# The router's two half-width products of a pair of channel blocks, side by side on TensorE's columns, with four places for x1

## The chip, the core and the metric

The kernel runs on one core of a Trainium2 chip. The metric is the device time of one execution in microseconds (us), as a median of several runs. The core's engines are PE (TensorE: matrix products), DVE (VectorE), ACT (ScalarE), POOL (GpSimd) and SP (SyncE, which here mostly issues transfers); PEld in the views is PE's loading of the stationary operand.

## What is computed

One layer of a decoder trunk over 2048 tokens of 1024 channels: a convolution module as token mixer, then a mixture of 32 gated-MLP experts, of which each token takes two, chosen by a router. Cut to what the change touches:

```
h   = rmsnorm(x, g1) * (1 + sc1) + sh1
u   = a * sigmoid(gt)            where a, gt = split(h @ w_in + b_in)
y   = silu(layernorm(depthwise_conv31(u) + b_dw)) @ w_out
x   = x + gate1 * y                                    # "x1" in the kernel
h   = rmsnorm(x, g2) * (1 + sc2) + sh2
grp_logits = h @ w_rg + b_rg     # 4 groups
exp_logits = h @ w_re + b_re     # 32 experts         -> 36 columns: "the router"
x   = x + gate2 * sum over the two chosen experts of p_e * (silu(h @ w_gate[e]) * (h @ w_up[e])) @ w_down[e]
out = rmsnorm(x, g3)
```

The kernel takes the router's products from the un-normalised x1 and applies the norm's factor afterwards to the 36 sums of each token (`finish`), so that the router can run while x1 is still being made, block of channels by block of channels.

## The kernel before, in words

**Tiling.** The 2048 tokens are cut into four chunks c = 0 to 3 of 512 tokens (`NCH`), the 1024 channels into eight blocks j = 0 to 7 of 128 (`KD`). The convolution's output product works on five pieces (`PIECES`): chunks 0, 1 and 2 whole, chunk 3 in two halves of 256 tokens. Channels lie on the 128 partitions and tokens along the free axis until the router is done; then the rows are written out by token, gathered by expert, and the experts run.

**Steps.** A loop over s = 8c + j issues for each step the input product of chunk c, block j (`conv_in`, 2 x 24 products of 128x128 by 512), the depthwise convolution of the block before (`dw`: some taps as column-tiled products on PE, L461, some on DVE, L490, some on ACT and POOL, L478 and L484), the layer norm of the chunk before (`layer_norm`), and, at the places that `PACE` gives, the output product of the chunk before (`conv_out`). The two halves of chunk 3 come at the end, all of `conv_out` of the one and then of the other, while the first expert's weights are being loaded. What is written is only a set of priorities: the order of each engine's instructions is set when the program is built, by a planner that runs a timeline of its own estimates, takes what is ready and prefers what is marked urgent. Each engine then works through its own list strictly in that order, and so does SP's list of transfers: a transfer whose place in memory isn't free yet holds all that stand behind it.

**conv_out (L542 to L562), one block j of one piece.** It takes a place for x1 and starts the load of the residual block into it (L548, 128 x 512 or 128 x 256 float32), runs 24 products into a PSUM bank (`gemm`, L388 to L390), adds the gated result to x1 on DVE (L552), transposes x1 on PE (L555), copies the transposed block out (L557 or L559), and runs the router's product of this block (L561): `wr2[:, j, :]`, 128 x 64 float32, as the stationary operand, x1 as the moving one. Even j accumulate in partitions 0 to 63 of the bank `lg`, odd j in partitions 64 to 127, so that each uses one half of PE's columns (`tile_position=(0, g)`). A float32 product of this kind stands in the trace as two records.

**Places.** x1 has two places in chunks 0 to 2 (`TMPB["x1"]`, 128 x 2 KB each), shared with the scratch tiles `junk`, `ls` and `zt` of `prep_norm`, `finish` and `mod_g2` (`JT`). In the two pieces of chunk 3 x1 takes its places from the pool "prod" instead (`X1E`), which has three. A place comes free when the router's product has read it.

**After the last block** `finish` copies `lg` out on ACT, adds the two halves on PE (L581, with the stacked identity `two`), and `routing` makes the choice; then come the experts (`Step`, L1111 and L1113).

Of the kernel before, what the change touches and what calls it, by code (L numbers as in the profile page):

```python
# [24 lines left out]
KD = D // P  # L25
# [69 lines left out]
MAXQ = max(q for t in TAPS for q, _ in t)  # L95
RW = CH + 4 * (MAXQ - 1)
WPB, WRB, UPB = 8, 1, 4
TMPB = {"acc2": 2, "prod": 3, "x1": 2}
BANKS = {"po": 1, "pa": 1, "pg": 1, "tr": 2, "lg": 1, "acc": 1, "out": 1}
LAG_DW, LAG_LN, LAG_OUT = 1, 2, 3  # L100
DELAY = 1
# [27 lines left out]
def moe_kernel(ctx, tc, x, xT, cols, ada, fing, w_in, w_out, b_r, wgu, wd, out):  # L129
    nc = tc.nc  # L130
# [76 lines left out]
    def pool(name, bufs=1, stack=None, **kw):  # L207
        return (stack or p1).enter_context(tc.tile_pool(name=name, bufs=bufs, reuse_waits="tile", **kw))
# [6 lines left out]
    grp = [pool("grp1")]  # L215
    sp = {tag: pool("sp_" + tag, n) for tag, n in TMPB.items() if tag != "x1"}
    rt4 = pool("rt4")
# [6 lines left out]

    sp["x1"] = pool("sp_x1", TMPB["x1"])
    mp = pool("mp")
# [7 lines left out]
    wr2 = c1.tile([P, KD, 64], F32, name="wr2")  # L234
# [13 lines left out]
    def urgent(offset=URGENT):  # L248
        return tc.high_priority(offset=offset)
# [4 lines left out]
    def bank(tag, name):  # L254
        return ps[tag].tile([P, 512], F32, tag=tag, name=name)

    def tmp(tag, name, shape=(P, 512), dt=F32):
        return sp[tag].tile(list(shape), dt, tag=tag, name=name)
# [85 lines left out]
    def parts(a):  # L344
        return a.rearrange("p (i q) -> p i q", q=P)
# [19 lines left out]
    def w_unit(c, src, dst, priority=WPRI, kept=0):  # L365

        with urgent(priority):
            h = wp.tile([P, D], F32R, tag="w", name="wh")
            l = wp.tile([P, D], F32R, tag="w", name="wl")
            if c <= kept:  # L370
                r = raw("wraw", src.tensor.name == w_in.tensor.name and c < 2)
                nc.sync.dma_start(r[:], src)
                S.activation(h[:], r[:], AF.Copy)
                V.tensor_tensor(l[:], r[:], h[:].bitcast(F32), op=OP.subtract)
                if c == kept:
                    nc.scalar.dma_start(dst[0], h[:].bitcast(F32))
                    nc.scalar.dma_start(dst[1], l[:].bitcast(F32))
            else:
                nc.sync.dma_start(h[:].bitcast(F32), dst[0])
                nc.sync.dma_start(l[:].bitcast(F32), dst[1])  # L380
            return h, l

    def gemm(po, w, xx, n):
        for k in range(KD):
            xh, xl = xx[k]
            wh, wl = (w[m][:, k * P:(k + 1) * P] if len(w) == 2 else w[2 * m + k // 4][:, k % 4 * P:(k % 4 + 1) * P]
                      for m in range(2))
            nc.tensor.matmul(po[:, :n], wh, xh[:, :n], start=(k == 0), stop=False)  # L388
            nc.tensor.matmul(po[:, :n], wh, xl[:, :n], start=False, stop=False)  # L389
            nc.tensor.matmul(po[:, :n], wl, xh[:, :n], start=False, stop=(k == KD - 1))  # L390
# [144 lines left out]
    def conv_out_tiles(c, o, n):  # L535
# [3 lines left out]
            xr = group("xr", 1)[:, :n // P, :]  # L539
        return xr, bank("lg" if o == 0 else "acc", "lg")  # L540

    def conv_out(c, o, n, j, z, xr, lg):  # L542

        end = c == NCH - 1
        w = wlast[j] if end else w_unit(c, w_out[j], (wo_d[0, j], wo_d[1, j]))
        x1 = tmp(X1E if end else "x1", "x1")
        with urgent(X1P):
            nc.sync.dma_start(x1[:, :n], xT[j][:, T0[c] + o:T0[c] + o + n])  # L548
        po = bank("pa" if end and j % 2 else "po", "po")
        gemm(po, w, z, n)  # L550
        with urgent():
            V.scalar_tensor_tensor(x1[:, :n], po[:, :n], modc[:, 16 + j:17 + j], x1[:, :n], op0=OP.mult, op1=OP.add)  # L552
            pb = bank("pg" if end and j % 2 else "out", "x1_t")
            for i in range(n // P):
                nc.tensor.transpose(pb[:, i * P:(i + 1) * P], x1[:, i * P:(i + 1) * P], ident[:])  # L555
            if j < XRV[c]:
                V.tensor_copy(xr[:, :, j * P:(j + 1) * P], parts(pb[:, :n]))  # L557
            else:
                S.activation(xr[:, :, j * P:(j + 1) * P], parts(pb[:, :n]), AF.Copy)  # L559
            g = 64 * (j % 2)  # L560
            nc.tensor.matmul(lg[g:g + 64, :n], wr2[:, j, :], x1[:, :n], start=(j < 2), stop=(j >= KD - 2),  # L561
                             tile_position=(0, g))  # L562

    def finish(c, o, n, xr, lg):

# [238 lines left out]
    def part(piece, j):  # L804
        conv_out(*piece, j, zs[piece], *outs[piece])
        if j == KD - 1:
            n = PIECES.index(piece)
            with urgent(FINISH[n]):
                L = finish(*piece, *outs[piece])
            with urgent(ROUTE[n]):  # L810
                return routing(*piece, L)
# [9 lines left out]
    for s in range(NS + LAG_OUT):  # L821
        c, j = divmod(s, KD)
# [47 lines left out]
    for m in g2t:  # L870
        w, n = P // m, D // m
# [478 lines left out]
```

## Time and profile before

| what | value |
|---|---|
| runs shown | 1604.31, 1604.81, 1607.11 us; median 1604.81 us |
| the profiled execution's own time | 1602.93 us |
| its span (first to last instruction) | 1601.2 us |
| PE busy | 1469.0 us, 92% of the span |
| DVE busy | 1120.2 us, 70% |
| ACT busy | 973.9 us, 61% |
| POOL busy | 741.2 us, 46% |
| DMA | 455.99 MB, 285 GB/s on average |
| granted TensorE clock, mean | 0.965 |

The share of an engine over the whole span is a mean over stages with different limits. The convolution fills about the first 800 us and the experts the rest. Busy times of PE are a union of records that overlap: the distance from one start to the next says more of a product's cost than its duration. "issue" as what ended an idle time means that the profile shows nothing that the engine waited for.

### The profile page before, as it was taken

What the parts mean: (1) busy time and instruction counts of PE and PEld (TensorE: products, weight loads), DVE (VectorE), ACT (ScalarE), POOL (GpSimd) and SP (SyncE); (2) the same over time, 40 slices, a digit from 0 to 9 for tenths busy, and PEclk for the clock granted to TensorE, in tenths of its full rate; (3) what the DMA queues carried; (4) which work ended last, traced back from release to release, by engine and by line L of the source; (5) the groups of instructions that cost most, each with busy time, mean ns of one, the idle gap of its engine ahead of it and who ended that gap; (6) DMA issues with size and microseconds to landing.
All of it is one profiled execution on the core that took longest, in us unless ns stands there. A gap on an engine that the chain in (4) does not pass through costs nothing.

```text
span 1601.2 us, 24058 instructions
## 1 busy us (share of the span) xinstructions
PE 1469.0 (92%) x8269; PEld 1067.6 (67%) x8269; DVE 1120.2 (70%) x1779; ACT 973.9 (61%) x1600; POOL 741.2 (46%) x564
## 2 busy tenths in 40 slices
PE   5989998999999999969887899998999999999984
PEld 4766676677777776648663465565778676866763
DVE  2659987788998898874462447334579787898465
ACT  4676788877868794444420435324477677876453
POOL 0378898887689977823241112122122222232322
PEclk8999999899999999979999999999999999999988
DMA  9699898666776665672649989989899889998987
GB/s 356 256 336 331 252 296 297 218 227 247 289 276 214 210 242 212 212 280 84 240 152 289 398 291 345 338 306 362 280 378 331 282 304 364 358 335 270 365 288 280
DMA packets 123647, 455.99 MB, mean 285 GB/s; under 512 B 25594, under 2 KB 29058, under 8 KB 98946
## 3 DMA queue, kind: packets, MB, share of 16 engines
q1 hardware_dynamic: 93842, 362.48, 62.9%
q0 software_dynamic: 14224, 40.43, 9.8%
q10 hardware_dynamic: 15456, 51.51, 8.2%
q8 instruction: 66, 1.08, 0.3%
q14 instruction: 59, 0.48, 0.1%
HBM read 374.24 MB, written 80.13 MB: 284 GB/s over the span
## 4 chain that ended last, share of the span: by engine, by line
PE 65%; DMA 14%; DVE 11%; issue 4%; ACT 4%; POOL 2%; SPq 1%; ACTq 0%; POOLq 0%; DVEq 0%
PE pg L1111 15%; PE pd L1111 8%; PE pg L1113 5%; DVE acc L490 4%; PE po L388 3%; PE po L389 3%; PE po L390 3%; PE pg L388 3%; PE pa L388 3%; PE pa L389 3%; PE pa L390 3%; PE pg L390 3%; PE pg L389 3%; DMA wraw<-in_wgu 2%; PE lg L561 2%
## 5 line engine op out<-in xcount | busy, mean ns | idle before, releaser
L484 POOL TENSOR_TENSOR acc<-acc,prod 128x512 f32<-128x512 f32 x321 | 430.4, 1341 | 52.3 <-ACT prod L478 30.8
L490 DVE SCALAR_TENSOR_TENSOR acc<-u,colt,acc 128x512 f32<-128x512 f32 x497 | 369.5, 750 | 21.8 <-PE acc L461 13.0
L1035 DVE TENSOR_TENSOR wl<-wraw,wh 128x1024 fp32r<-128x1024 f32 x260 | 308.0, 1227 | 74.3 <-ACT wh L1034 68.9
L478 ACT ACTIVATE prod<-u,colt 128x512 f32<-128x512 f32 x385 | 269.3, 721 | 109.3 <-POOL acc L484 83.3
L1034 ACT ACTIVATE wh<-wraw 128x1024 fp32r<-128x1024 f32 x264 | 264.0, 1057 | 108.1 <-PE pd L1111 46.1
L1111 PE MATMUL pg<-wh,xh 128*128 128x512 f32 x464 | 152.5, 401 | 10.0 <-issue 6.9
L1156 POOL DMA_INDIRECT x2acc<-ys,ft x24 | 64.1, 2671 | 195.4 <-DVE ys L1153 189.9
L1111 PE MATMUL pg<-wh,xl 128*128 128x512 f32 x464 | 149.4, 396 | 0.0
L1111 PE MATMUL pg<-wl,xh 128*128 128x512 f32 x464 | 148.7, 395 | 0.1
L1113 PE MATMUL pg<-wraw,xh 128*32 128x256 f32 (+1 forms) x992 | 124.0, 462 | 4.2 <-DMA wraw<-in_wgu 3.7
L388 PE MATMUL pg<-hh,wh 128*128 128x512 f32 x256 | 105.1, 411 | 20.6 <-ACT u L420 9.9
L1156 POOL DMA_INDIRECT x2acc<-ys,rt x20 | 33.7, 1685 | 184.0 <-DVE ys L1153 104.0
L1111 PEld LDWEIGHTS pg<-wh,xh 128*128 128x128 f32 x464 | 87.2, 190 | 33.0 <-issue 10.2
L1129 ACT ACTIVATE sg<-pg 128x256 f32<-128x256 f32 (+1 forms) x79 | 26.7, 369 | 129.9 <-PE pg L1113 74.4
L1080 ACT ACTIVATE psx<-psx,modc,A 128x128 f32<-128x128 f32 x232 | 89.4, 438 | 26.4 <-issue 15.7
L390 PE MATMUL pg<-hh,wl 128*128 128x512 f32 x256 | 104.0, 406 | 1.5 <-DMA wl<-wi_d 1.5
L389 PE MATMUL pg<-hl,wh 128*128 128x512 f32 x256 | 104.3, 407 | 0.7 <-DVE hl L350 0.7
L388 PE MATMUL pa<-hh,wh 128*128 128x512 f32 x256 | 101.4, 396 | 1.2 <-DVE u L425 0.6
L1111 PEld LDWEIGHTS pg<-wl,xh 128*128 128x128 f32 x464 | 87.8, 190 | 20.1 <-DVE wl L1035 0.9
L390 PE MATMUL pa<-hh,wl 128*128 128x512 f32 x256 | 101.1, 395 | 0.0
L389 PE MATMUL pa<-hl,wh 128*128 128x512 f32 x256 | 101.2, 395 | 0.0
L388 PE MATMUL po<-zz,wh 128*128 128x512 f32 (+1 forms) x256 | 96.3, 381 | 4.9 <-ACT zz L349 4.9
(279 smaller groups left out, 2888.3 us busy)
## 6 DMA issues: line engine op xcount, KB each, us to landing
wraw<-in_wgu SPq DMA_DIRECT2D x128, 1024.0 KB, 8.8
wraw<-in_wd SPq DMA_DIRECT2D x64, 1024.0 KB, 7.6
adar<-in_ada SPq DMA_DIRECT2D x44, 512.0 KB, 9.7
wh<-wi_d SPq DMA_DIRECT2D x42, 512.0 KB, 4.7
wl<-wi_d SPq DMA_DIRECT2D x42, 512.0 KB, 5.9
wraw<-in_w_in SPq DMA_DIRECT2D x22, 512.0 KB, 8.5
wh<-wo_d SPq DMA_DIRECT2D x20, 512.0 KB, 4.5
wl<-wo_d SPq DMA_DIRECT2D x20, 512.0 KB
```

Source lines behind the costliest of these rows:

```text
L388: nc.tensor.matmul(po[:, :n], wh, xh[:, :n], start=(k == 0), stop=False)
L389: nc.tensor.matmul(po[:, :n], wh, xl[:, :n], start=False, stop=False)
L390: nc.tensor.matmul(po[:, :n], wl, xh[:, :n], start=False, stop=(k == KD - 1))
L478: S.activation(pr[:, :n], u[:, k:k + n], AF.Copy, scale=wdw[:, k:k + 1])
L484: Q.tensor_tensor(acc2[:, :n], acc2[:, :n], pr[:, :n], op=OP.add)
L490: V.scalar_tensor_tensor(acc, u[:, k:k + n], wdw[:, k:k + 1], acc, op0=OP.mult, op1=OP.add)
L1034: S.activation(h[:, o], r[:, o], AF.Copy)
L1035: (Q if len(ws) == 1 and n % 3 == 2 else V).tensor_tensor(l[:, o], r[:, o], h[:, o].bitcast(F32), op=OP.subtract)
L1080: S.activation(ps[:, q, :], ps[:, q, :], AF.Identity, bias=modc[:, 24 + k:25 + k], scale=A2[:, k:k + 1])
L1111: nc.tensor.matmul(outs[o][:], st[x], mv, start=a, stop=z)
L1113: nc.tensor.matmul(outs[0][o * w:(o + 1) * w, :n], st[x], mv, start=a, stop=z, tile_position=(0, o * w))
L1156: d = Q.indirect_dma_start(out=x2acc[:].rearrange("t (m n) -> (t m) n", m=s.m), out_offset=bass.IndirectOffsetOnAxis(ap=s.si, axis=0), in_ ...
```

## The change

`conv_out` no longer runs the router's product of block j at once. It keeps x1 in a dictionary, and at every odd j runs the two products of blocks j - 1 and j directly one after the other, the even one on the left half of PE's columns, the odd one on the right half. x1 gets four places instead of two in chunks 0 to 2; the pool "prod", from which chunk 3 takes its x1, keeps three. Number, shapes and operands of the products stay as they were.

```diff
-TMPB = {"acc2": 2, "prod": 3, "x1": 2}
+TMPB = {"acc2": 2, "prod": 3, "x1": 4}
...
+    routed = {}
+
     def conv_out(c, o, n, j, z, xr, lg):
...
-            g = 64 * (j % 2)
-            nc.tensor.matmul(lg[g:g + 64, :n], wr2[:, j, :], x1[:, :n], start=(j < 2), stop=(j >= KD - 2),
-                             tile_position=(0, g))
+
+            routed[j] = x1
+            for q in (j - 1, j) if j % 2 else ():
+                g = 64 * (q % 2)
+                nc.tensor.matmul(lg[g:g + 64, :n], wr2[:, q, :], routed.pop(q)[:, :n], start=(q < 2), stop=(q >= KD - 2),
+                                 tile_position=(0, g))
```

## Rows read from the trace of the kernel before

**Rows 1.** The page: busy us of each engine, share of the span, records.
```profile
PE 1469.0 (92%) x8269; PEld 1067.6 (67%) x8269; DVE 1120.2 (70%) x1779; ACT 973.9 (61%) x1600; POOL 741.2 (46%) x564
```
**Rows 2.** Busy time by stretch: stretch, length, each engine's busy us, clock, DMA share, GB/s.
```profile
240.00:280.00 40.00, 34.23 (x169) 26.46 (x167) 31.09 (x44) 32.43 (x56) 35.51 (x28) 0.99 0.90 296
...
440.00:480.00 40.00, 38.34 (x212) 29.33 (x212) 39.47 (x80) 24.30 (x42) 33.28 (x26) 1.00 0.76 280
480.00:520.00 40.00, 40.00 (x190) 30.70 (x191) 35.84 (x53) 35.28 (x60) 37.06 (x29) 1.00 0.62 210
...
720.00:760.00 40.00, 39.66 (x301) 34.83 (x299) 16.38 (x55) 18.89 (x41) 12.56 (x14) 1.00 0.26 84
```
**Rows 3.** The chain that ended last, at 419 us: start, us, what.
```profile
419.15 0.61 ACT zz L349
419.78 0.69 DVE zz L350
```
**Rows 4.** PE's timeline, one router product of 512 tokens and the next product.
```profile
293.55 1.07 PE L561 MATMUL lg<-x,wr 128*64 128x512 f32 x2
294.55 0.50 PE L388 MATMUL po<-zz,wh 128*128 128x512 f32 x1
```
**Rows 5.** The router's line: durations in ns min/median/max, first and last start.
```profile
L561 PE MATMUL lg<-x,wr x80: 379/592/1116, 293.6 to 794.3; 128*64 128x512 f32 x48, 128*64 128x256 f32 x32
```
**Rows 6.** PE's timeline, products on quarters and halves of the columns.
```profile
234.46 1.04 PE L461 MATMUL acc<-R,Wd 128*32 128x512 f32 x2
236.14 1.06 PE L461 MATMUL acc<-R,Wd 128*32 128x512 f32 x6
297.28 1.06 PE L461 MATMUL acc<-R,Wd 128*32 128x512 f32 x8
864.14 3.65 PE L1113 MATMUL pg<-wraw,xh 128*64 128x512 f32 x16
```
**Rows 7.** PE's timeline, router products of 256 tokens: the first; a later one and what follows.
```profile
726.47 0.65 PE L561 MATMUL lg<-x,wr 128*64 128x256 f32 x2
...
775.72 0.65 PE L561 MATMUL lg<-x,wr 128*64 128x256 f32 x2
776.30 0.39 PE L388 MATMUL po<-zz,wlast 128*128 128x256 f32 x1
```
**Rows 8.** The chain that ended last, from 660 to 695 us.
```profile
660.12 1.00 PE lg L561 x2
...
663.03 5.21 DMA u_d<-u
...
669.58 6.01 DMA R<-u_d
...
689.38 5.94 DVE acc L490 x9
```
**Rows 9.** The last piece: transfers issued by SP, then the waits of DVE and PE.
```profile
764.36 4.74 SPq L1023 DMA_DIRECT2D wraw<-in_wgu  x4
770.46 1.45 SPq L548 DMA_DIRECT2D x<-in_xT  x2
776.40 0.33 SPq L548 DMA_DIRECT2D x<-in_xT  x1
784.68 0.88 DVE L552 SCALAR_TENSOR_TENSOR x<-po,modc,x 128x256 f32<-128x256 f32 x2 [4.79 <-DMA x<-in_xT]
785.31 0.66 PE L555 MATMUL x_t<-ident,x 128*128 128x128 f32 x2 [4.79 <-DVE x L552]
```
**Rows 10.** PE's idle time at 282 us and what ended it.
```profile
282.32 0.76 PE L388 MATMUL pg<-hh,wh 128*128 128x512 f32 x1 [6.21 <-DMA wh<-wi_d]
```
**Rows 11.** SP's waits, 250 to 830 us: us in total, times, longest.
```profile
SPq L548 <- PE lg L561: 34.4, 19, 3.7
```
**Rows 12.** Time to landing of the x1 loads (L548), all forty.
```profile
DMA to landing us min/median/max: 2.8/3.5/5.7
```
**Rows 13.** Splitting of the first experts' weights on DVE, 760 to 835 us.
```profile
L1035 DVE TENSOR_TENSOR wl<-wraw,wh x8: 1205/1219/3422, 774.1 to 816.2; 128x1024 fp32r<-128x1024 f32 x8
```

## The prediction, made before the result was known

> **What bounds the kernel now.** I read the page first: PE is busy for 92% of the span [rows 1]. Such a mean hides the stages, so next I took the busy times in stretches of 40 us. In the convolution, where the router's products lie (294 to 794 us [rows 5]), PE is full in some stretches while the others have room: 40.00 of 40 us at 480 us against 35.84 on DVE and 37.06 on POOL, and 39.66 at 720 us with DVE at 16.38. Elsewhere the roles are reversed: at 440 us DVE has 39.47 and PE 38.34 [rows 2]. So a microsecond off PE is worth up to a microsecond in the former, and less in the latter. PE's timeline then gives prices, the chain of waits shows the places where PE isn't the one that sets the pace, and SP's timeline shows what the loads do.
>
> **What the change removes.** The work doesn't shrink: 24 products of 512 tokens and 16 of 256 remain (two records each [rows 5]). What can go is time on PE, where each even block's product now runs alone. Such a visit costs, from its start to that of the next product, 294.55 - 293.55 = 1.00 us with 512 tokens [rows 4] and 776.30 - 775.72 = 0.58 us with 256 [rows 7]. If both halves of the columns work at once, the even visit disappears: 12 pairs at 1.00 and 8 at 0.58, 16.6 us of PE time.
>
> Do halves work at once? No row of before shows the router's pair itself; three rows bound it. One tap on four quarters, eight records and four times the work of a lone quarter, takes 1.06 us [rows 6], the 1.07 us of one lone router product [rows 4]. The experts' products on halves, in the very form 128x64 by 512, take 3.65 us for 16 records, that is four pairs at 0.91 us [rows 6], less than one lone visit. The upper bound is two visits, 2.0 us: no gain. I take one visit for the pair, since the rows of the same form say so.
>
> The Trainium skill speaks against this: "TensorE: Matmul & The Clock Gate", Part 3, "The mechanism", says that a weight load overlaps running products only where the row groups differ, and two column halves use the same rows. By that rule the second half would wait for the first, the pair would cost two visits, and the sum below would be zero. The trace disagrees: the tap's eight weight loads and eight products fit into 1.06 us [rows 6].
>
> **How much of it lies on the path.** By stage, the even visits only:
>
> Chunk 0 (294 to 414 us), four visits, 4.0 us. PE's list is nearly gapless there, but what follows is a stretch on DVE. It opens at 419 us with a split that ACT releases [rows 3], after chunk 0's last block and its `finish`; DVE then has 0.53 us free in 40 [rows 2]. That opening follows PE, so it comes earlier too, yet DVE must also have done its earlier taps sooner. The bounds are 0 and 4.0; I take 3.0, nearer to the upper end as DVE waited just ahead of it.
>
> Chunk 1 (471 to 577 us), four visits, 4.0 us. PE is full and DVE has 4.2 us free in 40, POOL 2.9 [rows 2]; one visit in some 27 us (the stage's 106 us by four pairs) is 1.5 us in 40, less than either. The first visit lies at the end of the DVE stretch, and finite places couple the engines. Bounds 2.0 and 4.0; 3.0.
>
> Chunk 2 (620 to 700 us), four visits. Blocks 0 and 2 come before the last u is stored at 663 us, 2.0 us. Blocks 4 and 6 come after, where the chain runs over the store (5.21 us), the loads of R (6.01 us) and nine taps on DVE (5.94 us) [rows 8]; PE waits there, and their 2.0 us buy nothing. Bounds 1.0 and 4.0; 2.0.
>
> Chunk 3 (726 to 794 us), eight visits of 0.58 us. The first half and blocks 0 and 2 of the second lie where PE has 39.66 us of 40 [rows 2]: 6 x 0.58 = 3.5 us. Block 4's visit lies ahead of a wait of 4.79 us for an x1 load [rows 9], which takes over what is saved: 0. Block 6's 0.58 us comes after it, among products that need loads of their own; I leave it out. Bounds 0 and 4.1.
>
> The sum is 3.0 + 3.0 + 2.0 + 3.5 = 11.5 us; with every upper end it is 4.0 + 4.0 + 4.0 + 4.1 = 16.1, with every lower end 3.0. What comes after 800 us moves as a block, since the routing starts from the last router product and the experts' weights from places that PE frees.
>
> **What the change adds.** No instruction. An even block's product now waits for the odd block's x1, but behind it in PE's list would stand only work that the odd block's own transposes already hold up, so PE gets no new wait. `finish` needs the odd product of block 7 last, as before.
>
> The x1 tiles stay longer. In chunks 0 to 2 the four places hold a pair in use and a pair on its way; today x1 loads wait 34.4 us in SP's list for the router's products [rows 11]. A load lands within 5.7 us [rows 12] and a pair's period is some 27 us, so this is covered. SP's list stands still less often; I give this nothing. Two more x1 loads may be started early, near 281 us, where PE already waits 6.21 us for weights [rows 10]: at 296 GB/s [rows 2] 256 KB take 0.9 us, so 0 to 1.8 us lost, if they go ahead of those weights. I take 0, since the weights were asked for earlier.
>
> In chunk 3 three places remain. The load of block j + 3 (j even) must now wait for the pair (j, j + 1), one block later than today. From there it has two blocks of PE work, some 8 us (12 blocks pass between 726.47 and 775.72 us [rows 7], 4.1 us each), and lands within 5.7 us: covered, if nothing stands ahead of it. Block 7 of the last piece waits for the pair (4, 5), after the wait at 785 us; it would be asked for near 787 us instead of 776.40 [rows 9] and land near 790 to 793, when PE ends the products ahead of it, near 793. This cover is thin; without it each microsecond late costs one, up to 3, which is part of chunk 3's bounds.
>
> **The rivals.**
>
> *The others take over.* POOL's 37.06 and DVE's 39.47 us of 40 [rows 2] say that the convolution is balanced: if they set the pace in chunks 0 and 1, these give 1.0 us each instead of 3.0, and the whole is 11.5 - 4.0 = 7.5, less 2 us for a planner whose other order fits less well: 5.5 us, 1599.3 us. For it speaks the DVE stretch; against it that PE waits so little between 480 and 600 us.
>
> *No pair.* The halves don't overlap, as by the skill's rule, or the planner puts other products between them, as it did with one tap, two records at 234.46 us and six at 236.14 [rows 6]. Then nothing changes: 1604.8 us. Against it speak the rows above; most taps stand unbroken.
>
> *Slower: the weights behind x1 in SP's list.* Today SP issues the first expert's weights at 764.36 us and the last three x1 loads after them [rows 9]. These x1 loads now depend on pairs. If the planner puts all of them ahead of the weights, the weights wait in SP's list until the pair (4, 5) of the last piece is done. Without the wait of 4.79 us that would be near 779 us: the weights come 779 - 764.4 = 14.6 us later, the 4.79 us are regained, and of the eight splits on DVE [rows 13] some five, 1.2 us each, fall into the routing that follows on DVE: 14.6 - 4.8 + 6 = 15.8 us. Against the 11.5 gained that is 4.3 us slower, 1609.1 us. It decides once the load of block 7 stands before the weights; with blocks 5 and 6 alone ahead, the loss is some 2 us and the sum stays a gain. Against it: the loads become free later than today, which moves them back in the list, not forward, and the weights are marked more urgent.
>
> **How the numbers follow.** The profiled execution took 1602.93 us, 1.9 below the median of the runs, 1604.81. 1602.93 - 11.5 = 1591.4 there; against the median 1593.3 us. Chances: forecast 0.58, others take over 0.18, no pair 0.11, slower 0.13. The range: the fastest is 1604.8 - 16.1 = 1588.7, to which the loads in SP's list might add a little, so 1588; at the top it takes in the second case and the third, 1604.8, and the spread of a median, 1606, and leaves most of the slower case out. The measurement can tell about 0.2% (3.2 us) from no change. Faster by more than that holds the forecast and nearly all of the second case, 0.74; the same is the third and a rest, 0.12; slower 0.14.
>
> **What would show it.** Right: L561's records in PE's timeline stand as four in about 1.06 us (0.65 with 256 tokens), and no L561 follows an even block's transposes; PE's busy time in the convolution falls by 14 to 17 us; the last router product comes some 11 us earlier than 794.3 us [rows 5]; the stretch behind it keeps its length. The stage terms can be read from the times at which chunk 0's, 1's and 2's last router products start. Wrong: if pairs take 2 us, if DVE's waits vanish and PE's grow by as much as the visits gave, if L548 waits in SP's list with L1023 behind it, or if PE waits longer than 4.79 us for x1 in the last piece. Wrong in another way: a gain up to 794 us that the experts don't keep.

## The result and the profile after

The changed kernel takes 1616.77 us (median of 7 runs, 1610.94 to 1618.91), the kernel before 1603.99 us (7 runs beside them, 1595.78 to 1607.11). The ratio is 1.0081, 95% interval 1.0062 to 1.0100: about 13 us **slower**, where 11.5 us faster was forecast. The profiled execution of the changed kernel took 1617.8 us, its span is 1616.0 us.

The page after, busy us of each engine, answers [rows 1]:

```profile
PE 1474.3 (91%) x8269; PEld 1070.5 (66%) x8269; DVE 1118.4 (69%) x1779; ACT 976.8 (60%) x1600; POOL 732.9 (45%) x564
```

PE was to lose 14 to 17 us of busy time; it has 5 us more. The router's line in PE's timeline says why (its number is L566 now), with the rows that answer [rows 4]:

```profile
301.80 0.60 PE L557 MATMUL x_t<-ident,x 128*128 128x128 f32 x4
302.33 1.07 PE L566 MATMUL lg<-x,wr 128*64 128x512 f32 x2
303.33 0.50 PE L388 MATMUL po<-zz,wh 128*128 128x512 f32 x1
...
317.43 1.07 PE L566 MATMUL lg<-x,wr 128*64 128x512 f32 x2
```

The view of that line after, which answers [rows 5]:

```profile
L566 PE MATMUL lg<-x,wr x80: 379/592/1116, 302.3 to 813.2; 128*64 128x512 f32 x48, 128*64 128x256 f32 x32
```

Block 0's product of two records stands behind its own transposes, and block 1's 15.1 us later: **no pair was formed**, here or in the other 19 places. The products are written next to each other, but the planner makes PE's order: the even block's product is ready as soon as its x1 is, and it is taken then. What is left of the change is the four places.

Those moved the work long before the first x1 exists. The scratch tile of the squares of `prep_norm`, L336, takes its places from x1's. ACT's timeline near 91 us, before:

```profile
89.63 1.04 ACT L336 ACTIVATE junk<-xs 128x1024 bf16<-128x1024 f32 x1
90.67 1.04 ACT L336 ACTIVATE junk<-xs 128x1024 bf16<-128x1024 f32 x1
92.32 0.67 ACT L420 ACTIVATE u<-pg,bh 128x512 f32<-128x512 f32 x1
92.89 1.04 ACT L336 ACTIVATE junk<-xs 128x1024 bf16<-128x1024 f32 x1
95.16 1.04 ACT L336 ACTIVATE junk<-xs 128x1024 bf16<-128x1024 f32 x1
```

The same after:

```profile
90.73 1.04 ACT L336 ACTIVATE junk<-xs 128x1024 bf16<-128x1024 f32 x1
91.77 1.04 ACT L336 ACTIVATE junk<-xs 128x1024 bf16<-128x1024 f32 x1
92.81 1.04 ACT L336 ACTIVATE junk<-xs 128x1024 bf16<-128x1024 f32 x1
93.85 1.04 ACT L336 ACTIVATE junk<-xs 128x1024 bf16<-128x1024 f32 x1
...
95.50 0.67 ACT L420 ACTIVATE u<-pg,bh 128x512 f32<-128x512 f32 x1
```

With two places two squares run, and the tanh that frees chunk 0's gate bank comes ahead of the other two; with four places all four run in a row, and the tanh comes behind them. From there the lists of all engines differ: chunk 1's transposes come earlier in PE's list, and the first of its 8269 records to stand in another place is the 573rd, at 103.65 us. PE's waits up to 300 us, before (line that waits, what it waits for, us in all, times, longest):

```profile
PE mod L303 <- DVE ms L267: 11.8, 1, 11.8
PE pg L388 <- ACT u L420: 9.9, 4, 5.7
PE pg L388 <- DMA wh<-wi_d: 6.2, 1, 6.2
PE mod L303 <- DMA adar<-in_ada: 2.3, 1, 2.3
```

The same after:

```profile
PE pg L388 <- ACT u L420: 12.4, 4, 8.0
PE mod L303 <- DVE ms L267: 11.1, 1, 11.1
PE xT L357 <- DMA R<-u_d: 9.6, 1, 9.6
PE mod L303 <- DMA adar<-in_ada: 5.2, 4, 2.6
```

The wait for the tanh is 8.0 us instead of 5.7; the wait near 282 us, 6.21 us for weights [rows 10], has become one of 9.58 us, of chunk 2's transposes, some 10 us later. All rows of this view together come to 36.5 and 43.2 us. The first router product starts at 302.33 instead of 293.55 us, chunk 0's last at 423.56 instead of 413.64, the last of all at 812.90 instead of 794.02. These are one profile of each kernel; the table further down shows how far two profiles of one list lie apart.

Two stretches that answer [rows 2], same columns:

```profile
480.00:520.00 40.00, 40.00 (x191) 30.89 (x190) 35.24 (x51) 34.42 (x56) 36.65 (x29) 1.00 0.46 155
720.00:760.00 40.00, 30.29 (x197) 25.67 (x198) 19.91 (x85) 21.00 (x36) 16.81 (x16) 0.77 0.36 127
```

PE is as full as before at 480 us. The last stretch holds other work now: what follows chunk 2's last router product, which starts at 714.91 us instead of 700.18, has moved into it, with its waits and a granted clock of 0.77. The last piece's transfers on SP, the wait of DVE and that of PE, answer [rows 9]:

```profile
784.07 4.14 SPq L1028 DMA_DIRECT2D wraw<-in_wgu  x4
...
789.37 1.65 SPq L550 DMA_DIRECT2D x<-in_xT  x2
...
795.51 0.33 SPq L550 DMA_DIRECT2D x<-in_xT  x1
803.62 0.87 DVE L554 SCALAR_TENSOR_TENSOR x<-po,modc,x 128x256 f32<-128x256 f32 x2 [4.63 <-DMA x<-in_xT]
804.25 0.66 PE L557 MATMUL x_t<-ident,x 128*128 128x128 f32 x2 [4.62 <-DVE x L554]
```

The order, weights first and the three x1 loads after them, and the wait of 4.6 us are those of before, some 19 us later.

### The profile page after: what moved, and what is told of

It is laid out like the page before. It is cut to its first block, busy times and chain, and to the rows that moved or that the text cites. A ratio compares the mean times of both kernels' runs of the same rounds, so it can differ in the third digit from the quotient of the medians.

```text
span 1616.0 us, 24042 instructions
## 1 busy us (share of the span) xinstructions
PE 1474.3 (91%) x8269; PEld 1070.5 (66%) x8269; DVE 1118.4 (69%) x1779; ACT 976.8 (60%) x1600; POOL 732.9 (45%) x564
## 3 DMA queue, kind: packets, MB, share of 16 engines
q8 instruction: 66, 1.08, 0.3%
## 5 line engine op out<-in xcount | busy, mean ns | idle before, releaser
L478 ACT ACTIVATE prod<-u,colt 128x512 f32<-128x512 f32 x385 | 268.3, 721 | 95.9 <-POOL acc L484 74.9
L1161 POOL DMA_INDIRECT x2acc<-ys,ft x24 | 57.0, 2375 | 187.8 <-DVE ys L1158 187.5
```

The source lines that it names most:

```text
L478: S.activation(pr[:, :n], u[:, k:k + n], AF.Copy, scale=wdw[:, k:k + 1])
L1161: d = Q.indirect_dma_start(out=x2acc[:].rearrange("t (m n) -> (t m) n", m=s.m), out_offset=bass.IndirectOffsetOnAxis(ap=s.si, axis=0), in_ ...
```

## The experiments

Three questions were put: which part of the change costs the 13 us, where in the program it acts, and what real pairs would have given. Ratios are to the kernel before, measured beside each kernel on the same chip, with 95% intervals. "The list" is the order of each engine's instructions in the built program.

**Which part.** The pair as it is written in the change, with two places:

```diff
+            routed[j] = x1
+            for q in (j - 1, j) if j % 2 else ():
...
```

> The changed conv_out with x1 back at two places. Theory (the pairs are never formed, because the planner takes the even block's product as soon as its x1 is there; the four places alone make the difference): every engine's list is that of the kernel before, 40 lone router products, and the time is that of before, ratio 1.000 within 0.002. Rival (holding x1 and asking for pairs costs time by itself): slower than before by a part of the 13 us, ratio 1.003 to 1.008.

1604.04 us, 0.9996 [0.9968, 1.0024], and the list of every engine is that of the kernel before. Writing two products next to each other does nothing here.

The four places alone:

```diff
-TMPB = {"acc2": 2, "prod": 3, "x1": 2}
+TMPB = {"acc2": 2, "prod": 3, "x1": 4}
```

> The kernel before with four places for x1 and nothing else. Theory (the places alone make the difference): the lists are those of the changed kernel, ratio 1.008 (about 13 us slower), and the first router product starts near 302 us instead of 293.6. Rival (the code of the pairs does it): ratio 1.000.

1615.76 us, 1.0058 [1.0035, 1.0081], with the list of the changed kernel. The whole loss belongs to this one number.

**Where the places act.** Four places of which two are held until some 427 us by the zero tile that is needed there anyway, so that only chunk 1's x1 and what follows have four:

```diff
+TMPB = {"acc2": 2, "prod": 3, "x1": 4}
...
+    zt = [tmp("x1", "zt") for _ in range(2)]
+    for h in range(2):
+        V.memset(zt[h][:], 0.0)
...
```

> The kernel before with four places for x1, of which two are taken by the zero tile of mod_g2 until about 427 us, so that chunk 1's squares find two places as before. The lists are those of before for the first 420 us. Theory (the loss comes in through chunk 1's squares alone): ratio 1.000 within 0.003, chunk 0's last router product near 413.6 us. Rival (four places cost time wherever they are, through the squares of later chunks or x1 loads ahead of weights): ratio 1.003 to 1.006, all of it after 420 us.

1603.96 us, 1.0001 [0.9979, 1.0023]. Up to 420 us its list is that of before. Four places for x1 itself, from chunk 1 on, cost nothing and give nothing.

Two places for x1, and two others that only chunk 1's third and fourth square use:

```diff
+TMPB = {"acc2": 2, "prod": 3, "x1": 2, "jk": 2}
...
-                junk = tmp(JT, "junk", (P, D), BF16)
+                junk = tmp("jk" if c == 1 and i > 1 else JT, "junk", (P, D), BF16)
```

> The kernel before with two places for x1, and two further places that only the last two of the four squares of chunk 1's norm use. Theory (the four places act first through the scratch tiles of these squares near 91 us, which moves chunk 1's transposes and with them the lists of all engines): the first router product starts near 302 us as in the changed kernel, 8 to 9 us later than before, and most of the 13 us are there, ratio 1.005 to 1.010. Rival (the loads of x1, which come near 281 us, or the places of later chunks do it): up to 280 us as before, ratio 1.000.

1616.29 us, 1.0079 [1.0054, 1.0104]. Two squares of 1.04 us that run earlier at 91 us bring the whole loss, without any change of x1's places. Up to 286 us its list is that of the changed kernel; behind that it is another one again.

Four places for all, but those two squares ordered behind the tanh of chunk 0's block 3 (the one that was late), and in a second kernel behind that of block 4 (`tanhs[4]`):

```diff
...
+                with tc.issue_after(tanhs[3].ins) if c == 1 and i > 1 else ExitStack():
+                    S.activation(junk[:], xs[:, i, :], AF.Square, accum_out=ss[:, i:i + 1])
```

> The kernel before with four places for x1, and one edge: chunk 1's last two squares stand behind the tanh of chunk 0's fourth block in ACT's list, as they do before. The squares then stand together behind it, so chunk 1's scaling and transposes still come earlier than before. Theory (the tanh behind two more squares costs the 2 to 3 us that PE waits more, the rest is the other list that follows): the wait of PE for this tanh is 5.7 us again, and the ratio lies at 1.002 to 1.007. Rival (the tanh is all): ratio 1.000.

> As the run with the tanh first, but behind the tanh of the fifth block: chunk 1's last two squares, its scaling and transposes come later than before, not earlier. Rival (what costs time is that chunk 1's preparation comes earlier, ahead of chunk 0's work): ratio at or under 1.000. Theory (the list of before is a good one among many, and any other that the planner falls into from here costs time): ratio 1.002 to 1.008.

The first: 1606.3 us, 1.0016 [0.9992, 1.0040]. Most of the loss is gone, though PE's wait for the tanh is still 8.0 us, where 5.7 was expected. The kernels with the list of before up to there have 5.5 to 7.1 us. So the tanh isn't the cost. The second: 1620.22 us, 1.0108 [1.0065, 1.0150], more than was expected, with a wait of 6.4 us: a shorter wait, and the slowest of these kernels. The loss goes with the list that follows from 91 us on; no single wait was found that carries it.

**What real pairs give.** Here the two products are ordered behind the transposes of the odd block, so that the even one can't be taken early. First in chunk 3 alone (`end`), with two places as before:

```diff
...
+                turned = nc.tensor.transpose(pb[:, i * P:(i + 1) * P], x1[:, i * P:(i + 1) * P], ident[:])
...
+            routed[j] = x1
+            for q in ((j - 1, j) if j % 2 else ()) if end else (j,):
+                g = 64 * (q % 2)
+                with tc.issue_after(turned.ins) if end else ExitStack():
+                    nc.tensor.matmul(lg[g:g + 64, :n], wr2[:, q, :], routed.pop(q)[:, :n], start=(q < 2), stop=(q >= KD - 2),
+                                     tile_position=(0, g))
```

> The kernel before with real pairs in the two pieces of chunk 3 alone: the products of both blocks may only be placed behind the odd block's transposes. The lists are those of before up to the first router product of chunk 3. Theory of the prediction's sum: a pair takes 0.58 to 0.66 us, the time of one, six visits of 0.58 us are saved ahead of the wait for x1, 3.5 us, ratio 0.998. Rival (three places are too few for pairs): the loads of x1 come a block later, PE waits for them, ratio 1.000 to 1.003. Rival (halves don't overlap): a pair takes 1.15 us and nothing is saved.

1598.64 us, 0.9987 [0.9969, 1.0005]. The same kernel again, with more runs:

> Real pairs in chunk 3 alone, once more with more rounds. From the first look: the chunk-3 stretch from chunk 2's last router product to the last one of all was 88 us instead of 94. Theory (PE alone sets the pace there): 3 to 6 us faster, ratio 0.9965 to 0.998. Rival (the routing behind it takes it back): ratio 1.000.

1598.15 us, 0.9969 [0.9950, 0.9988]. The two measurements overlap; together they say 2 to 5 us faster than before, the best of all kernels of this study. PE's timeline of the first of them shows the pairs, and the last piece's wait:

```profile
724.56 0.65 PE L567 MATMUL lg<-x,wr 128*64 128x256 f32 x4
...
777.52 0.66 PE L557 MATMUL x_t<-ident,x 128*128 128x128 f32 x2 [6.53 <-DVE x L554]
778.11 1.12 PE L567 MATMUL lg<-x,wr 128*64 128x256 f32 x4
...
785.07 0.41 PE L557 MATMUL x_t<-ident,x 128*128 128x128 f32 x2 [0.67 <-DVE x L554]
785.41 0.65 PE L567 MATMUL lg<-x,wr 128*64 128x256 f32 x4
```

Four records now take 0.65 us, as two did [rows 7]: the even visit is gone. From block 1 to the last block of chunk 3 it is 60.9 us here (724.56 to 785.41) and 60.5 to 60.7 in four of the other five kernels with pairs there, against 64.8 before (729.25 to 794.02) and 62.9 to 65.0 in nine of the ten other kernels without. The fifth with pairs, in all chunks and with two places, has 65.1, and its waits follow; the tenth without, with the squares behind block 4's tanh, has 67.8. Without these two the means are 60.7 and 64.0, some 3.3 us apart.

Pairs in all chunks, with two places, with four, and with the late four of above (`if end else ...` left out):

> Real pairs in all pieces (the products of both blocks may only be placed behind the odd block's transposes), x1 with two places. The lists are those of before up to the first router product. Theory of the prediction's sum: twelve visits of 1.00 us and eight of 0.58 us go, 11.5 us of it on the path, ratio 0.993, a pair takes 1.07 us. Rival (two places are too few: the load of the next pair starts only when this pair is done): PE waits for x1 at up to twelve pairs, 1 to 3 us each, ratio 1.000 to 1.015. Rival (DVE, ACT and POOL set the pace of the convolution): ratio 0.998 to 1.000 with PE's busy time lower by 16 us.

> The changed kernel with its pairs made real by the same edge, four places from the start. Theory (two independent effects): the 9 us that chunk 1's squares cost up to the first router product stay, the later part of the loss is another list's, and the pairs give some 11 us back: ratio 0.999 to 1.003. Rival (the loss is the price of pairs not formed): ratio 0.993.

> Real pairs in all pieces, four places for x1 of which two are taken by the zero tile until about 427 us. Theory of the prediction's sum: the list of before up to the first router product, the pairs' 11.5 us, and loads of x1 in time: ratio 0.993, faster than with two places by what those make PE wait. Rival (the other engines set the pace): ratio 0.998 to 1.000.

Two places: 1613.58 us, 1.0083 [1.0052, 1.0113]. Four: 1610.29 us, 1.0049 [1.0030, 1.0068]. Late four: 1604.02 us, 0.9994 [0.9975, 1.0014]. Four places from the start were expected at 0.999 to 1.003, if the pairs gave back 11 us of what the squares cost; they didn't. The router's line alone, before and with the late places (stretch, length, busy us of PE and of PEld, clock, DMA share, GB/s):

```profile
0.00:795.00 795.00, 37.87 (x80) 7.89 (x80) 0.97 0.74 254
0.00:798.00 798.00, 18.63 (x80) 4.06 (x80) 0.96 0.73 253
```

With two places it is 19.27 us. So half of the router's time on PE is gone, some 19 us of its records, and no gain shows in the run. All of PE up to the start of the last router product, the same 4240 records or so, is busy for 730.08 us before, 721.21 with two places and 717.53 with late ones: 9 and 13 us less. A cut at a fixed time would mislead here: up to 840 us PE is busy for 754.86 and 755.26 us in these two kernels and for 769.96 before, but for 757.26 with four places alone, which has no pair; it has merely got less far by then.

With two places, PE's longest wait from 290 to 800 us says where a part went (9.7 us before, same view):

```profile
PE x_t L557 <- DVE x L554: 17.6, 7, 7.3
```

PE waits for x1, whose loads wait in SP's list for the router's products, 50.7 us from 250 to 830 us and up to 12.8 at once, where it was 34.4 and 3.7 [rows 11]. With the late places that wait in SP's list is about as long, 49.8 and 11.6, so places alone don't end it. PE's three longest there (9.7, 2.6 and 1.9 before):

```profile
PE x_t L560 <- DVE x L557: 11.3, 4, 7.3
PE tT L530 <- ACT t L525: 7.5, 2, 7.0
PE pg L391 <- DMA wh<-wi_d: 6.0, 4, 2.4
```

**Chunk by chunk**, with the late places and the edge in one chunk (`c == 0`, `c == 1`, `c == 2`), then in two (`c in (1, 3)`):

```diff
...
+            for q in ((j - 1, j) if j % 2 else ()) if c == 1 else (j,):
...
+                with tc.issue_after(turned.ins) if c == 1 else ExitStack():
...
```

> The kernel with the late four places and real pairs in chunk 0 alone, where x1 has two places. The prediction's term: four visits of 1.00 us, 3.0 us on the path (bounds 0 and 4.0), ratio 0.998. Theory now (pairs in chunk 0 put the planner onto another list from the first router product, and the convolution behind it is balanced): the pairs' gain is lost, ratio 1.000 to 1.006, with chunk 0's last router product later than without pairs.

> The kernel with the late four places (ratio 1.000 as measured) and real pairs in chunk 1 alone, the stage in which PE's busy time was 40.00 of 40 us. The prediction's term: four visits of 1.00 us go, 3.0 us of it on the path (bounds 2.0 and 4.0), ratio 0.998. Rival (DVE, ACT and POOL, at 35 to 37 of 40 us, set the pace as soon as PE has room, or the even block's wait holds them up): ratio 1.000 to 1.003, PE's waits in 480 to 600 us grow by what the visits gave.

> The kernel with the late four places and real pairs in chunk 2 alone. The prediction's term: 2.0 us on the path (bounds 1.0 and 4.0), ratio 0.9988. Theory now (the chain runs over the store of u, the loads of R and DVE's taps): ratio 0.999 to 1.002; chunk 2's last router product is at most 1 us earlier.

> The kernel with the late four places and real pairs in chunks 1 and 3, the two stages in which PE is full and the others have room. If the terms add: 2.4 us from chunk 1 and 5.0 us from chunk 3 as measured one by one, ratio 0.9955, the fastest version. Rival (another list behind chunk 1's pairs takes it back): ratio 0.998 to 1.000.

Chunk 0: 1615.42 us, 1.0070 [1.0047, 1.0093]. Chunk 1: 1599.23 us, 0.9985 [0.9963, 1.0006]. Chunk 2: 1604.31 us, 1.0000 [0.9980, 1.0020]. Chunks 1 and 3: 1601.85 us, 0.9991 [0.9969, 1.0012].

Chunk 0's loss is a list again. The stretch from 370 to 420 us in the kernel with late places and no pairs:

```profile
370.00:420.00 50.00, 49.86 (x263) 38.35 (x262) 44.26 (x72) 37.53 (x60) 39.61 (x34) 1.00 0.58 203
```

And in that with pairs in chunk 0:

```profile
370.00:420.00 50.00, 44.75 (x225) 34.27 (x225) 40.63 (x65) 32.07 (x50) 36.57 (x30) 0.93 0.52 189
```

PE has 225 records instead of 263 in the same 50 us, and all other engines do less as well: none is full. SP's waits from 290 to 420 us may be a part of it (without the pairs the first line is 14.9, 5, 4.5, and the second isn't among the seven longest):

```profile
SPq L375 <- DVE wl L377: 27.9, 5, 17.5
SPq L298 <- PE mod L303: 24.4, 3, 15.0
SPq L553 <- PE lg L570: 14.8, 3, 9.1
```

Loads of weights to be split (L375) and of the modulation's weights (L298) hold SP's list for up to 17.5 us at once; without the pairs the longest hold is 9.6 us, of x1's loads for transposes. Over the whole stretch SP's list stands still about as long in both, 111 us: the holds are longer and fewer, not more in all. That they are the cause isn't shown.

The stages, in us between the last router products of the chunks, from one profile each ("rest" is from the last router product to the end of the execution's own time):

| kernel | chunk 0's last at | chunk 1 | chunk 2 | chunk 3 | rest |
|---|---|---|---|---|---|
| before | 413.6 | 162.7 | 123.8 | 93.8 | 808.9 |
| written pair, two places (same list) | 418.4 | 162.9 | 122.8 | 92.9 | 805.4 |
| late places | 417.6 | 160.2 | 123.6 | 96.1 | 807.6 |
| after | 423.6 | 165.3 | 126.1 | 98.0 | 804.9 |
| four places alone (same list as after) | 425.7 | 166.7 | 126.4 | 90.8 | 811.2 |
| chunk 1's squares early | 424.6 | 166.1 | 122.2 | 93.3 | 807.7 |
| pairs in chunk 0 | 420.4 | 166.2 | 120.6 | 95.9 | 809.8 |
| pairs in chunk 1 | 415.3 | 155.1 | 124.8 | 92.3 | 808.0 |
| pairs in chunk 2 | 417.6 | 160.0 | 122.8 | 94.2 | 813.7 |
| pairs in chunk 3 | 412.5 | 162.8 | 121.9 | 88.1 | 809.0 |
| pairs in chunks 1 and 3 | 412.3 | 155.2 | 125.5 | 92.8 | 812.7 |
| pairs in all, two places | 418.0 | 164.5 | 128.1 | 89.6 | 811.8 |
| pairs in all, four places | 418.0 | 160.5 | 128.6 | 92.7 | 824.1 |
| pairs in all, late places | 420.1 | 165.9 | 116.6 | 94.1 | 803.8 |

Two profiles of one list differ by up to some 7 us in a stage (chunk 3, after and four places alone; the first column, 412.5 and 419.2 in the two profiles with pairs in chunk 3). So single cells say little. What stands out over several is where the loss of 13 us comes in: chunk 0's last router product lies at 424 to 426 us in the three kernels without pairs whose squares run early, and at 412 to 419 in the eight profiles with the list of before up to there, some 9 us earlier in the mean; chunk 1 then takes 165 to 167 us against 160 to 163 in those of the eight without pairs in it, another 4. With the squares behind block 3's tanh, where most of the loss is gone, chunk 0's last lies at 418.3 again.

Chunk 1's 155 stands out too, in both kernels with pairs there and none in chunk 0; with pairs in all chunks it is 160 to 166. Chunk 3's 88.1 (88.3 in the second profile of that kernel) is the shortest, but the other kernels with pairs there have 89.6 to 94.1, little less than those without (90.8 to 98.6).

## Why the prediction was wrong

**The step that failed first:** "If both halves of the columns work at once, the even visit disappears". The hardware half of it holds. What failed is the half that wasn't argued: that two products that stand next to each other in the program stand next to each other in PE's list. The text had said that the order is a planner's; it counted that only as a rival, "No pair", where the planner puts other products between. It is more than that: the planner had no reason to hold the even product back at all, since in chunk 0 it runs 12 to 24 us before its partner does (the first two pairs start at 302.33 and 317.43 us, 329.81 and 353.90 us). The kernel with the written pair and two places gives that rival's time, 1604.8, within the noise: 1604.04.

**The step that made it slower:** "SP's list stands still less often; I give this nothing", and 0 to 1.8 us for early loads. The places were costed as places for x1. The front of the text says that `junk`, `ls` and `zt` share them, and the squares that use `junk` were not followed. This is the term that was mis-sized, 0 against a loss of some 13 us. Even as costed it missed: SP's wait for the router's products, 34.4 us [rows 11], is 43.3 us in the changed kernel, no less.

**The rivals.** None had the mechanism of the loss. "The weights behind x1 in SP's list" ended on the right side, with 1609.1 us, but its mechanism isn't in the trace: the weights stand ahead of the three x1 loads, as before. That the side came out right was luck. "The others take over" is the nearest to what the kernels with real pairs in all chunks show, and more strongly than priced: with late places 13 us less on PE up to the last router product, and 0.9994 [0.9975, 1.0014]. Whether the other engines set the pace there, or another list brings other waits, the runs don't separate.

**The terms, as the kernels with real pairs measured them:**

- PE's time: the price was right, since one pair takes the time of one product: 0.65 us with 256 tokens, as above, and with 512 1.01 us to the next product, where one took 1.00 [rows 4]. The router's own records lose 19 us. PE as a whole, of which 14 to 17 us were forecast, loses 9 with two places and 13 with late ones up to the last router product; two kernels with one list (after and four places alone) lie 7 us apart there, 738.42 and 731.60. The rule of the Trainium skill ("TensorE: Matmul & The Clock Gate", Part 3, "The mechanism") on weight loads, as the prediction applied it, would have made a pair cost two products. The traces of these kernels disagree with it, as the tap in [rows 6] did; the last section has the pair's weight loads.
- Chunk 3, 3.5 us: 3.9 us from block 1 to the last against the profile of before, 3.3 us between the means of the two groups of kernels. The stage of that one profile is 5.7 us shorter, more than eight visits of 0.58 us can give, so this isn't the pairs alone. "Block 4's visit lies ahead of a wait of 4.79 us" held: the wait is 6.53 us with pairs. The load of block 7 was asked for after the pair, and its cover, called thin, held but for 0.67 us.
- Chunk 1, 3.0 us: the stage is 5 to 8 us shorter, more than its four visits of 1.00 us can give, so a part of that is another list. The whole run is 0.0015 of the time shorter, 2.4 us, with an interval that holds zero: it fits the term, but doesn't show it beyond the noise.
- Chunk 2, 2.0 us: no gain is seen, 1.0000 [0.9980, 1.0020]; the interval, 3.2 us to either side, can't rule the 2.0 out.
- Chunk 0, 3.0 us: a loss of 11 us. The reason given, that DVE's stretch follows PE, didn't get its test, since the list ahead of it was another one.
- The sum: the terms don't add. Chunks 1 and 3 together give less than either alone by the medians, and the interval, from 0.9969 on, leaves out the 0.9955 of their sum. In that kernel's profile both gains are there (155.2 us in chunk 1, 60.5 us from block 1 of chunk 3 to the last); what takes them back lies elsewhere and wasn't found.

**What stays open:** why the lists that the planner makes from another order at 91 us, or from pairs in chunk 0, are worse ones. That they are is shown, by kernels with the same instructions in another order. Of the reasons, the single wait for the tanh was tried and falls, and that the steps behind 91 us come late doesn't explain it either: with the squares behind block 4's tanh the u of step s = 14 starts earlier than before (272.9 against 279.9 us), and that kernel is the slowest. The rest, some us of waits in each stage, was not separated.

## What to carry to other kernels

Where a planner orders the instructions, look at its list before counting on two of them standing side by side; if they must, say so with an ordering edge, and only in a stage where the engine that is relieved sets the pace alone. Before giving a pool more places, follow every tile that shares the pool, in the whole program. And take into the sum that any edit that moves the list in a balanced stage may cost several us by itself, 13 here with not one instruction changed; an edit that takes effect late in the program puts less of it at risk. Here the pairs of chunk 3, the last, were the only ones whose gain stood clear of the noise, in the second of two measurements.

## What the runs showed of the hardware

Two float32 products on the two halves of the columns cost PE the time of one. That was expected from [rows 6], and is now shown for this very pair; with 512 tokens in PE's timeline of the kernel with pairs in all chunks and late places, and the pair's weight loads:

```profile
490.69 0.20 PEld L570 LDWEIGHTS lg<-x,wr 128*64 128x64 f32 x4 [0.17 <-issue]
490.69 1.08 PE L570 MATMUL lg<-x,wr 128*64 128x512 f32 x4
491.70 0.50 PE L392 MATMUL pa<-hl,wh 128*128 128x512 f32 x1
```

All four weight loads are done 0.20 us after the start, while the products run for 1.08.

Not expected was what a wait for x1 costs beyond itself. The kernel with pairs in chunk 3, around its wait of 6.53 us (the columns of [rows 2]):

```profile
766.00:771.00 5.00, 4.99 (x43) 4.79 (x40) 3.07 (x5) 4.99 (x12) 2.38 (x2) 1.00 1.02 425
771.00:777.00 6.00, 0.00 (x0) 0.00 (x0) 0.81 (x2) 1.07 (x2) 0.96 (x1) 0.68 0.86 337
777.00:780.00 3.00, 2.48 (x10) 1.43 (x11) 0.76 (x2) 0.38 (x1) 0.00 (x0) 0.50 0.02 8
780.00:783.00 3.00, 3.00 (x16) 3.00 (x16) 1.08 (x1) 0.00 (x0) 0.00 (x0) 0.50 0.19 44
```

PE is idle from 771 to 777 us, and the granted clock is 0.50, the lower of its two levels (1.2 GHz), for the 6 us after it; the pair at 778.11 takes 1.12 us there instead of 0.65. The kernel before shows the same behind its wait of 4.79 us: 0.50 from 785 to 791 us. Six microseconds of work at half the clock are about three lost, an estimate from these rows: the wait that the pairs left in place costs some 9 us and not 6.5, more than the pairs of chunk 3 brought.
